# Order of loads and of the first q products in a diffusion layer, with idle matmuls between

## The chip, the cores and the metric

One core of a Trainium2 chip. The metric is the device time of one execution in microseconds; lower is better. Five engines work side by side, each through its own queue in order: TensorE (PE; its weight loads are listed as PEld), VectorE (DVE), ScalarE (ACT), GpSimd (POOL) and SyncE (SP), which here issues nearly all DMA transfers.

## The reference

One layer of a transformer with adaptive norms, in fp32, on 128 context tokens and 512 latent tokens (640 in all), model width 1024:

- `mod = silu(cond) @ w_ada + b_ada` gives, for each of two condition vectors (context, latent), six vectors of 1024: shift, scale and gate for the mixer, and the same for the FFN.
- `h = rms(x, norm_mix) * (1 + sc1) + sh1`.
- `h @ w_in` is cut into q (512 columns), k and v (128 each) and three blocks of 512 for a gated short convolution.
- Attention on normed, rotated q and k; the convolution beside it; both normed, concatenated and put through `w_out`; a gated residual.
- The same modulation for a SwiGLU FFN of 2816 with a gated residual.
- Outputs: both token sets, and k and v of the context tokens.

Only the part up to `h @ w_in` for the q columns is touched by the change.

## The kernel before

All matmuls that need fp32 accuracy are done as three products of rounded parts: a value is split into a high part (`hi`, rounded to the fast fp32r form) and a low part (`lo = value - hi`), and `mm3` (lines 150 to 153) adds hi·hi, hi·lo and lo·hi. `split` (146 to 148) rounds on ScalarE and subtracts on VectorE. The split of the modulated tokens is `hH`, `hL`; that of the weights `wh`, `wl`.

**The first stage** (to about 63 us) makes `h` for all tokens and the q products. Model width is cut into eight blocks k of 128. For the stage these things are needed:

- `x_norm(t)` (`r` in the list, 470 to 475): for token tile t of 128 tokens, ScalarE squares and sums, VectorE makes `ms` (line 159), GpSimd takes the power -0.5 (161), VectorE scales x (475).
- `xT_do(t)` (`x`): eight turns (transposes) of x on TensorE into PSUM, and two copies of 512 columns out of it into `xT`, on ScalarE or VectorE as `XTE` says. For the first `XB` tiles both halves lie in one double PSUM tile, for the others in two single ones.
- `ada1_mm(k)` (`a`): the adaLN product for block k, eight small matmuls with the condition vectors (`cp`, 32 columns, of which two are used) as the stationary side. `cp` is set to zero on GpSimd (332); its two live columns are copied on VectorE (369) from `cs`, which comes from a turn of the SiLU of the conditions (362 to 366). VectorE copies the result out (`res`, 418).
- `ada1_mod(k)` (`m`): four tiny matmuls on `res` and then three small VectorE instructions (399, 400, 403) give scale `modA` and shift `modB` of block k.
- `h_do(k, cc)` (`h`): ScalarE makes `hF = modA * xT + modB` for the 512 latent tokens, VectorE for the 128 context tokens, then `split` makes `hH` and `hL`.
- `load_split` (`w`): the split of a loaded pair of q weight blocks (1024 columns).
- `q_mm(k, t)` (`q`): three matmuls of 512 columns that add block k to the q product of token tile t; five PSUM banks hold the sums over all k.

The order is written out. `P1PRE` is a list of these steps that is run first; while it is traced, VectorE, ScalarE and GpSimd keep exactly its order (`pre_order`), and so does TensorE (`pe_order`, from ahead of it to the end of the kernel). It ends with modulated blocks 0 and 1 and all q products of k = 0. Then a loop over k from 1 runs `P1SEQ`: modulation of k+1, `h` of k+1, adaLN product of k+2, and the five q products of k. In the loop the other engines are ordered by the planner of the language, by its own costs and by program order.

**Loads.** SyncE issues them. `LOADS` gives the first ones: 0 is the next x tile (512 KB), a positive number that many steps of the adaLN loads (a block k is two loads of two pieces, 1 MB, in two of the four `af` buffers; a third step hands the block over), -1 the next weight of the stream `order` (q weights, four pairs of 512 KB, then kv, then the convolution's). The buffers of block k come free when `ada1_mm(k-2)` is done. Further weights are issued when a product asks for its own (`W`, 252 to 261): it loads up to `AHEAD` = 3 places further. SyncE's order is the planner's.

**After it** follow the kv products, attention with the convolution between, the output projection and the FFN; TensorE's order in them is written out too (`SEQ`). They are not edited.

Of the kernel before, what the change touches and what calls it, by code (L numbers as in the profile page):

```python
# [30 lines left out]
EPS = 1e-6  # L31
CG = 32
SOQ = [0, -300, -300, -300]
P1SEQ = 'm h a 0 1 2 3 4'
P1PRE = ('r0 r1 r2 x0 r3 x1 v0 x2 a0 w0 x3 m0 r4 h00 a1 q02 q01 x4 q00 m1 h01 h10 a2 q03 h11 p0 q04 c0')
XB = 3
XTE = [0, 1, 0, 1, 1, 1, 0, 1, 1, 0]
SEQ = ('k1 c0 q4 k4 C0 k0 K4 Q4 q0 a0 F1 k2 a1 K0 t0 k3 t1 o0 K1 F1 Q0 o1 K2 F1 K3 F1 S0.0 F1 F1 S0.1 '
# [16 lines left out]
AOP = 9  # L55
# [18 lines left out]
AO = 6  # L74
# [6 lines left out]
AHEAD = 3  # L81
OSQ = 2
AFB = 4
LOADS = [0, 0, 0, 0, 2, 1, -1, 0, 3, 3, 2, 2]
O_Q, O_K, O_GB, O_GC, O_U = 0, 512, 768, 1280, 1792


def build(ctx, tc, x_prompt, x_sample, c, cache_k, cache_v, c_ctx, norm_mix, norm_ffn, w_ada, b_ada,
# [3 lines left out]
    act, dve, pool, pe, sp = nc.scalar, nc.vector, nc.gpsimd, nc.tensor, nc.sync  # L92
# [23 lines left out]
    def T(tag, shape, dt=F32, bufs=1):  # L116
        seq[0] += 1
        return pools[where.get(tag, "A")][1].tile(list(shape), dt, tag=tag, bufs=bufs, name=f"{tag}_{seq[0]}")

    def PB(shape=(P, 512), dt=F32, tag="t"):  # L120
        seq[0] += 1
        if kept.get(tag):
            w = kept[tag].pop()
            n = 1
            for y in shape[1:]:
                n *= y
            w = w[:, :n] if tag != "s" else w
# [12 lines left out]
    def f32(ap):  # L140
        return ap.bitcast(F32)
# [4 lines left out]
    def split(hi, lo, src):  # L146
        act.activation(hi, src, AF.Copy)  # L147
        dve.tensor_tensor(lo, src, f32(hi), ALU.subtract)  # L148
# [81 lines left out]
    deferred = []  # L230
    in_pre = [False]

    def load_split(e, wf):
        key, src, ph, ring, gain, _ = e
        a, b = src.shape[1], src.shape[2]
        wh = T(ring + "h", (P, a, b), F32R, WHB)
        wl = T(ring + "l", (P, a, b), F32R, WHB)
        if gain is None:
            with early(SOQ[key[1]] if key[0] == 'q' else SOW):
                split(wh, wl, wf)  # L240
        else:
            for i in range(a):
                g = vec[:, gain + i:gain + i + 1]
                act.activation(wh[:, i], wf[:, i], AF.Copy, scale=g)
                dve.scalar_tensor_tensor(wl[:, i], wf[:, i], g, f32(wh[:, i]), ALU.mult, ALU.subtract)
        e[5] = (wh, wl)

    def load_next(later=False):
        load(order[stream_at[0]], later)
        stream_at[0] += 1  # L250

    def W(key):
        p = place[key]
        while not in_pre[0] and stream_at[0] < len(order):
            nxt = order[stream_at[0]][0][0]
            ahead = AO if nxt == "o" else AOP if nxt in ("g", "u", "op") else AHEAD
            if stream_at[0] > p + ahead or order[stream_at[0]][2] > phase[0]:
                break
            load_next()
        assert order[p][5] is not None, key  # L260
        return order[p][5]
# [33 lines left out]
    for gi, grp in enumerate(GROUPS):  # L295
# [5 lines left out]
        for j in range(2):  # L301
            for i0 in range(0, len(grp), 2):
                n = len(grp[i0:i0 + 2])
# [3 lines left out]
                        plan(("ada", 5, 1, kp), wa[:, 2 * kp:2 * kp + 2, 5 * D + 512:6 * D], 2, "f")  # L307


    crow = T("crow", (16, P))  # L310
    sp.dma_start(crow[0:8, :], c[0].rearrange("(r q) -> r q", q=P))
    sp.dma_start(crow[8:16, :], c_ctx.rearrange("(r q) -> r q", q=P))
# [13 lines left out]
    ident = T("ident", (P, P))  # L326
# [4 lines left out]
    cp = T("cp", (P, KD, CG))  # L331
# [14 lines left out]
    def ada1_next(n):  # L346
        for _ in range(n):
            next(loads, None)
# [41 lines left out]
    modA = [T(f"modA{i}", (P, KD, 2)) for i in range(2)]  # L390
# [19 lines left out]
    def ada1_mm(k):  # L410
        while k not in ada1:
            ada1_next(1)
        rp = PB((P, 256), tag="c")
        for h, wf in enumerate(ada1[k]):
            for i in range(4):
                cond_mm(rp, 4 * h + i, wf[:, i].rearrange("p a b -> p (a b)"))
        res = T("res", (P, 256), F32, 2)
        dve.tensor_copy(res, rp)
        ada1[k] = res
# [8 lines left out]
    xT = T("xT", (P, KD, TOK))  # L428
# [21 lines left out]

    hF = {}

    def h_do(k, cc):
        if k not in hF:
            hF[k] = T("hF", (P, TOK), F32, 2)
        s = (slice(0, 512), slice(512, TOK))[cc]
        a, b = modA[0][:, k, cc:cc + 1], modB[0][:, k, cc:cc + 1]
        if cc == 0:
            act.activation(hF[k][:, s], xT[:, k, s], AF.Identity, bias=b, scale=a)
        else:  # L460
            dve.tensor_scalar(hF[k][:, s], xT[:, k, s], a, b, ALU.mult, ALU.add)
        if k == 0:
            split(hH[k][:, s], hL[k][:, s], hF[k][:, s])
        elif cc == 1:
            split(hH[k], hL[k], hF[k])

    pe_order = tc.manual_schedule(engines={mybir.EngineType.PE})
    pe_order.__enter__()

    def x_norm(t):  # L470
        junk = T2((P, D), mybir.dt.bfloat16)
# [37 lines left out]
    steps = {"r": x_norm, "c": late_consts, "w": lambda i: load_split(*deferred.pop(0)), "p": lambda i: rows2_load(), "x": xT_do, "v": lambda i: (vec_do, vec2_do)[i](), "m": ada1_mod, "a": ada1_mm}  # L509
    pre_order = tc.manual_schedule(engines={mybir.EngineType.DVE, mybir.EngineType.Activation, mybir.EngineType.Pool})  # L510
    pre_order.__enter__()
    in_pre[0] = True
    for x in P1PRE.split():
        k = int(x[1])
        if x[0] == "h":
            h_do(k, int(x[2]))
        elif x[0] == "q":
            q_mm(k, int(x[2]))
        else:
            steps[x[0]](k)  # L520
# [3 lines left out]
    sp.dma_start(ck, cache_k[0, 0])  # L524
    cv = T("cv", (P, NKV, HD))
    sp.dma_start(cv, cache_v[0, 0])
    for k in range(1, KD):
        ada1_next(3)
        for x in P1SEQ.split():
            if x == "m" and k + 1 < KD:  # L530
                ada1_mod(k + 1)
            elif x == "h" and k + 1 < KD:
                h_do(k + 1, 0)
                h_do(k + 1, 1)
            elif x == "a" and k + 2 < KD:
                ada1_mm(k + 2)
            elif x.isdigit():
                q_mm(k, int(x))
        if k == 2:
            vec2_do()  # L540

    qraw = [None] * NT
    for t in (CTX, 0, 1, 2, 3):
        qraw[t] = T("of", (P, 512), F32, NT)
# [751 lines left out]
```

## Time and profile before

| | |
|---|---|
| median of 3 runs | 761.24 us (761.2 to 762.45) |
| the profiled execution | 762.03 us, span in the profile 760.3 us |
| mean granted clock of TensorE in it | 0.995 |
| busy, share of span | PE 97%, DVE 74%, ACT 49%, POOL 6% |
| DMA | 84.5 MB, mean 111 GB/s; 291, 289, 258 GB/s in the first three fortieths (57 us) |

How to read the lines quoted below. A line of a group names the source line, the engine, the instruction, the tiles (out<-in), the shapes and the count; then busy time in total and mean ns of one; then the engine's idle time ahead of them and who ended it. A line of the timeline begins with the start and the duration in us. `[5.55 <-ACT t L473]` says the engine sat idle 5.55 us until that instruction released it. A line of the chain has the start, the time that the chain spent in it, and what it was. Matmuls overlap one another, so a duration is longer than the distance to the next.

### The profile page before, as it was taken

The page shows a single profiled execution, that of the slowest core. Times are in us where ns is not written, and L with a number is a line of the kernel's source. Part 1 is how long each engine was busy: PE and PEld are TensorE (multiplying, and loading weights), DVE is VectorE, ACT ScalarE, POOL GpSimd, SP SyncE. Part 2 cuts the span into 40 slices and gives each one's busy share as a digit, 9 for nine tenths or more (in the row PEclk, how much of TensorE's full clock was granted, in tenths as well). Part 3 has the DMA queues.
Part 4 walks back from the last instruction along what each step waited for, and adds up shares of the span by engine and source line. Part 5 has one row for each costly group of instructions (what it writes and reads, how often), then busy time and mean ns, then how long its engine had stood idle before and what let it go on. Part 6 is the DMA issues. An engine that isn't in the chain of part 4 may idle for free.

```text
span 760.3 us, 11889 instructions
## 1 busy us (share of the span) xinstructions
PE 738.2 (97%) x4580; PEld 663.4 (87%) x4580; DVE 559.1 (74%) x1009; ACT 373.6 (49%) x713; POOL 48.7 (6%) x77
## 2 busy tenths in 40 slices
PE   4999999999999999999999999999999999999997
PEld 3778988989999887799998789998889998899986
DVE  5556987676567799799879678875578866788653
ACT  5355776666555445865552135552125541255410
POOL 2104201011010130000000000000000000000000
PEclk9899999999999999999999999999999999999999
DMA  9994133423423453031325223223113132232312
GB/s 291 289 258 138 43 111 110 155 91 106 159 91 117 156 199 112 1 111 56 112 90 176 85 66 98 81 90 111 52 56 111 57 111 80 60 87 81 112 55 84
DMA packets 102349, 84.52 MB, mean 111 GB/s; under 512 B 4526, under 2 KB 82674, under 8 KB 102292
## 3 DMA queue, kind: packets, MB, share of 16 engines
q1 hardware_dynamic: 100980, 83.39, 36.1%
q8 instruction: 36, 0.59, 0.3%
q10 hardware_dynamic: 1056, 0.26, 0.2%
q14 instruction: 21, 0.17, 0.1%
q0 software_dynamic: 256, 0.11, 0.1%
HBM read 79.68 MB, written 2.75 MB: 108 GB/s over the span
## 4 chain that ended last, share of the span: by engine, by line
PE 80%; DVE 9%; ACT 3%; DMA 3%; issue 2%; SPq 1%; POOL 1%; POOLq 0%; DVEq 0%; ACTq 0%
PE pf L151 17%; PE pf L152 17%; PE pf L153 17%; PE pc L674 3%; PE pc L675 3%; PE pc L676 3%; PE ps L788 2%; PE po L831 2%; PE pt L814 2%; PE ps L151 2%; DMA af<-in_w_ada_dram 2%; PE pc L376 2%; PE ps L152 2%; PE ps L153 2%; POOL rs L161 1%
## 5 line engine op out<-in xcount | busy, mean ns | idle before, releaser
L147 ACT ACTIVATE wh<-wf 128x1024 fp32r<-128x1024 f32 (+1 forms) x76 | 64.2, 844 | 92.7 <-PE pf L153 63.1
L151 PE MATMUL pf<-wh,gT 128*128 128x512 f32 (+1 forms) x225 | 88.1, 391 | 0.0
L152 PE MATMUL pf<-wl,gT 128*128 128x512 f32 (+1 forms) x225 | 87.7, 390 | 0.0
L153 PE MATMUL pf<-wh,gT 128*128 128x512 f32 (+1 forms) x225 | 87.6, 390 | 0.0
L148 DVE TENSOR_TENSOR wl<-wf,wh 128x1024 fp32r<-128x1024 f32 (+1 forms) x42 | 49.3, 1174 | 28.1 <-ACT wh L147 25.2
L674 PE MATMUL pc<-hH,wh 128*128 128x320 f32 x192 | 61.1, 318 | 0.0
L676 PE MATMUL pc<-hH,wl 128*128 128x320 f32 x192 | 59.4, 309 | 0.0
L675 PE MATMUL pc<-hL,wh 128*128 128x320 f32 x192 | 59.3, 309 | 0.0
L151 PEld LDWEIGHTS pf<-wh,gT 128*128 128x128 f32 x225 | 42.2, 188 | 9.9 <-ACT wh L147 0.2
L152 PEld LDWEIGHTS pf<-wl,gT 128*128 128x128 f32 x225 | 42.2, 188 | 9.9 <-issue 0.2
L153 PEld LDWEIGHTS pf<-wh,gT 128*128 128x128 f32 x225 | 42.2, 188 | 9.8
L151 PE MATMUL pf<-T,wh 128*128 128x320 f32 x160 | 49.3, 308 | 1.5 <-ACT p L1129 1.5
L151 PE MATMUL pf<-T,wl 128*128 128x320 f32 x160 | 49.2, 308 | 0.0
L152 PE MATMUL pf<-T,wl 128*128 128x320 f32 x160 | 49.2, 308 | 0.0
L153 PE MATMUL pf<-T,wl 128*128 128x320 f32 x160 | 49.2, 308 | 0.0
L152 PE MATMUL pf<-T,wh 128*128 128x320 f32 x160 | 49.2, 308 | 0.0
L153 PE MATMUL pf<-T,wh 128*128 128x320 f32 x160 | 49.2, 307 | 0.0
L151 PE MATMUL pf<-B,wl 128*128 128x320 f32 x152 | 46.9, 308 | 0.0
L152 PE MATMUL pf<-B,wl 128*128 128x320 f32 x152 | 46.8, 308 | 0.0
L153 PE MATMUL pf<-B,wl 128*128 128x320 f32 x152 | 46.8, 308 | 0.0
L1208 DVE TENSOR_TENSOR dm<-pf,g 128x512 f32<-128x512 f32 (+1 forms) x41 | 27.7, 675 | 23.1 <-PE pf L153 23.1
L147 ACT ACTIVATE wl<-wf 128x512 fp32r<-128x512 f32 x34 | 21.4, 630 | 43.5 <-PE pf L152 36.8
(282 smaller groups left out, 2055.7 us busy)
## 6 DMA issues: line engine op xcount, KB each, us to landing
wf<-in_w_gate_up_dram SPq DMA_DIRECT2D x44, 512.0 KB, 4.0
aw<-in_w_ada_dram SPq DMA_DIRECT2D x24, 512.0 KB, 4.8
wf<-in_w_down_dram SPq DMA_DIRECT2D x20, 512.0 KB, 3.4
wf<-in_w_in_dram SPq DMA_DIRECT2D x18, 512.0 KB, 5.7
af<-in_w_ada_dram SPq DMA_DIRECT2D x32, 256.0 KB, 5.8
x<-in_x_sample_dram SPq DMA_DIRECT2D x8, 512.0 KB, 5.2
wf<-in_w_out_dram SPq DMA_DIRECT2D x8, 512.0 KB, 4.7
wf<-in_w_ada_dram SPq DMA_DIRECT2D x8, 512.0 KB, 3.8
```

The lines of the kernel that those rows point to most:

```text
L147: act.activation(hi, src, AF.Copy)
L148: dve.tensor_tensor(lo, src, f32(hi), ALU.subtract)
L151: pe.matmul(out, lh, rh, start=start, stop=False, skip_group_check=more)
L152: pe.matmul(out, lh, rl, start=False, stop=False, skip_group_check=more)
L153: pe.matmul(out, ll, rh, start=False, stop=stop, skip_group_check=more)
L376: pe.matmul(out[CG * g:CG * (g + 1)], cp[:, k], w, start=(k < 4), stop=(k >= KD - 4), skip_group_check=True)
L674: pe.matmul(acc, wh[:, k], hH[k][:, c0:c0 + n], start=(k == 0), stop=False)
L675: pe.matmul(acc, wh[:, k], hL[k][:, c0:c0 + n], start=False, stop=False)
L676: pe.matmul(acc, wl[:, k], hH[k][:, c0:c0 + n], start=False, stop=(k == KD - 1))
L788: pe.matmul(s2[:, g, :320], q, kk[:, v, P + g * 320:P + (g + 1) * 320], start=(i == 0), stop=(i == 1))
L814: pe.transpose(tp[:, i, h], u[3][h][:, kt * P:(kt + 1) * P], ident)
L1208: dve.tensor_tensor(dm, ps[:, :n], g2[cc][:, oc], ALU.mult)
```

## The change

- The list `P1PRE` is new. It begins with eight **idle products** (`d8`: `spin`, matmuls of `ident` with all 256 columns of `cp` into a PSUM tile that nobody reads); six more stand singly between its steps. It takes the q products of k = 0 by token tiles as their tokens get ready: `h` of block 0 is made in four parts (tiles 0 and 1, tile 2, tile 3, context). The q products of k = 1 are in the list as well, and `h` of block 2. The norms of x tiles 2, 3 and 4 stand later in it, between these.
- The loop starts at k = 2; its order is adaLN product of k+1, two q products, modulation of k+1, `h` of k+1, three q products. The adaLN product is thus one block ahead, not two.
- `h_do`: ScalarE rounds `modA * xT + modB` straight into `hH`; VectorE makes the fp32 `hF` for all tokens, and subtracts.
- `LOADS`: two x tiles, adaLN block 0, the first q weights, two x tiles, block 1, the context's x tile, block 2, the second q weights, block 3. The third and fourth q weights are issued in the loop behind the adaLN blocks 5 and 7; products no longer load q weights ahead.
- SyncE and TensorE keep the written order from the first transfer on, to the end of the loop.
- Two double PSUM tiles of x instead of three (`XB`), and other engines for its copies (`XTE`).

```diff
-P1SEQ = 'm h a 0 1 2 3 4'
-P1PRE = ('r0 r1 r2 x0 r3 x1 v0 x2 a0 w0 x3 m0 r4 h00 a1 q02 q01 x4 q00 m1 h01 h10 a2 q03 h11 p0 q04 c0')
-XB = 3
-XTE = [0, 1, 0, 1, 1, 1, 0, 1, 1, 0]
+P1SEQ = 'a 0 1 m h 2 3 4'
+P1PRE = ('d8 r0 r1 x0 v0 x1 d1 a0 d1 m0 d1 w0 h0a r2 d1 q00 q01 r3 x2 d1 h0b a1 q02 x3 d1 m1 h0c h1l q03 r4 q10 q11 x4 a2 '
+         'q12 q13 h04 h14 m2 w0 h2* q04 q14 p0 c0')
+XB = 2
+XTE = [0, 1, 0, 1, 0, 1, 0, 1, 0, 1]
...
-LOADS = [0, 0, 0, 0, 2, 1, -1, 0, 3, 3, 2, 2]
+LOADS = [0, 0, 2, 1, -1, 0, 0, 3, 0, 3, -1, 3]
...
-            ahead = AO if nxt == "o" else AOP if nxt in ("g", "u", "op") else AHEAD
+            ahead = AO if nxt == "o" else 0 if nxt == "q" else AOP if nxt in ("g", "u", "op") else AHEAD
...
+    sp_order = tc.manual_schedule(engines={mybir.EngineType.SP, mybir.EngineType.PE})
+    sp_order.__enter__()
...
+    HS = {"a": slice(0, 256), "b": slice(256, 384), "c": slice(384, 512), "l": slice(0, 512), "4": slice(512, TOK)}
+
+    def h_do(k, part):
         if k not in hF:
             hF[k] = T("hF", (P, TOK), F32, 2)
-        s = (slice(0, 512), slice(512, TOK))[cc]
-        a, b = modA[0][:, k, cc:cc + 1], modB[0][:, k, cc:cc + 1]
-        if cc == 0:
-            act.activation(hF[k][:, s], xT[:, k, s], AF.Identity, bias=b, scale=a)
-        else:
-            dve.tensor_scalar(hF[k][:, s], xT[:, k, s], a, b, ALU.mult, ALU.add)
-        if k == 0:
-            split(hH[k][:, s], hL[k][:, s], hF[k][:, s])
-        elif cc == 1:
-            split(hH[k], hL[k], hF[k])
-
-    pe_order = tc.manual_schedule(engines={mybir.EngineType.PE})
-    pe_order.__enter__()
+        for x in "l4" if part == "*" else part:
+            s, cc = HS[x], int(x == "4")
+            g, b = modA[0][:, k, cc:cc + 1], modB[0][:, k, cc:cc + 1]
+            act.activation(hH[k][:, s], xT[:, k, s], AF.Identity, bias=b, scale=g)
+            dve.tensor_scalar(hF[k][:, s], xT[:, k, s], g, b, ALU.mult, ALU.add)
+            if part != "*":
+                dve.tensor_tensor(hL[k][:, s], hF[k][:, s], f32(hH[k][:, s]), ALU.subtract)
+        if part == "*":
+            dve.tensor_tensor(hL[k], hF[k], f32(hH[k]), ALU.subtract)
+
+    def spin(n):
+        w = PB((P, 256))
+        for _ in range(n):
+            pe.matmul(w, ident, cp.rearrange("p a b -> p (a b)"), start=True, stop=True)
...
-    for k in range(1, KD):
+    for k in range(2, KD):
         ada1_next(3)
+        if k in (3, 5):
+            load_next()
         for x in P1SEQ.split():
             if x == "m" and k + 1 < KD:
                 ada1_mod(k + 1)
             elif x == "h" and k + 1 < KD:
-                h_do(k + 1, 0)
-                h_do(k + 1, 1)
-            elif x == "a" and k + 2 < KD:
-                ada1_mm(k + 2)
+                h_do(k + 1, "*")
+            elif x == "a" and k + 1 < KD:
+                ada1_mm(k + 1)
             elif x.isdigit():
                 q_mm(k, int(x))
-        if k == 2:
+        if k == 3:
             vec2_do()
 
+    sp_order.__exit__(None, None, None)
+    pe_order = tc.manual_schedule(engines={mybir.EngineType.PE})
+    pe_order.__enter__()
```

More of the change, by code (lines that the diff above doesn't have):

```diff
@@ L451, in build @@
     hF = {}
-    def h_do(k, cc):
+    HS = {"a": slice(0, 256), "b": slice(256, 384), "c": slice(384, 512), "l": slice(0, 512), "4": slice(512, TOK)}
+    def h_do(k, part):
         if k not in hF:
             hF[k] = T("hF", (P, TOK), F32, 2)
-        s = (slice(0, 512), slice(512, TOK))[cc]
-        a, b = modA[0][:, k, cc:cc + 1], modB[0][:, k, cc:cc + 1]
-        if cc == 0:
-            act.activation(hF[k][:, s], xT[:, k, s], AF.Identity, bias=b, scale=a)
-        else:
-            dve.tensor_scalar(hF[k][:, s], xT[:, k, s], a, b, ALU.mult, ALU.add)
-        if k == 0:
-            split(hH[k][:, s], hL[k][:, s], hF[k][:, s])
-        elif cc == 1:
-            split(hH[k], hL[k], hF[k])
-    pe_order = tc.manual_schedule(engines={mybir.EngineType.PE})
-    pe_order.__enter__()
+        for x in "l4" if part == "*" else part:
[11 more added lines that the diff above has]
+            pe.matmul(w, ident, cp.rearrange("p a b -> p (a b)"), start=True, stop=True)
     def x_norm(t):
@@ L507, in rows2_load @@
         pool.dma_start(rows2[8:20, :], conv_w[0].rearrange("w (r q) -> (w r) q", q=P))
-    steps = {"r": x_norm, "c": late_consts, "w": lambda i: load_split(*deferred.pop(0)), "p": lambda i: rows2_load(), "x": xT_do, "v": lambda i: (vec_do, vec2_do)[i](), "m": ada1_mod, "a": ada1_mm}
+    steps = {"r": x_norm, "c": late_consts, "w": lambda i: load_split(*deferred.pop(0)), "p": lambda i: rows2_load(), "x": xT_do, "d": spin, "v": lambda i: (vec_do, vec2_do)[i](), "m": ada1_mod, "a": ada1_mm}
     pre_order = tc.manual_schedule(engines={mybir.EngineType.DVE, mybir.EngineType.Activation, mybir.EngineType.Pool})
@@ L515, in build @@
         if x[0] == "h":
-            h_do(k, int(x[2]))
+            h_do(k, x[2])
         elif x[0] == "q":
```

## The prediction

> **What bounds the kernel now.** I read the page first, then the chain of waits in order of time, then the busy time by stretches, then the instructions of the first 75 us one by one, and last the groups by shape.
>
> ```profile
> span 760.3 us, 11889 instructions
> PE 738.2 (97%) x4580; PEld 663.4 (87%) x4580; DVE 559.1 (74%) x1009; ACT 373.6 (49%) x713; POOL 48.7 (6%) x77
> af<-in_w_ada_dram SPq DMA_DIRECT2D x32, 256.0 KB, 5.8
> ```
>
> TensorE is busy nearly throughout, so a gain must come from where it waits or runs at half clock. Only the first 63 us are edited. Two rows of the chain of waits in that part, and the stretches (busy us of each engine, granted clock, DMA share, GB/s), cut where the granted clock changed:
>
> ```profile
> 11.84 7.41 DMA af<-in_w_ada_dram
> ...
> 32.50 8.34 DMA af<-in_w_ada_dram
> ```
>
> ```profile
> core 0: us, PE busy (x) PEld busy (x) DVE busy (x) ACT busy (x) POOL busy (x), PEclk, DMA share, GB/s
> 8.30:11.70 3.40, 3.40 (x16) 3.22 (x16) 2.11 (x4) 2.43 (x5) 1.10 (x2) 1.00 1.16 309
> ...
> 15.10:18.50 3.40, 1.24 (x13) 0.71 (x12) 3.02 (x8) 2.14 (x5) 0.27 (x1) 1.00 1.20 294
> 18.50:21.90 3.40, 2.51 (x12) 1.44 (x13) 1.87 (x3) 1.13 (x2) 3.27 (x6) 0.50 1.20 290
> 21.90:25.30 3.40, 3.40 (x14) 2.91 (x13) 0.69 (x1) 0.23 (x1) 0.00 (x0) 0.50 1.20 283
> ...
> 34.20:62.90 28.70, 27.96 (x174) 20.86 (x174) 15.14 (x36) 13.06 (x16) 1.43 (x2) 1.00 0.93 262
> ```
>
> Up to 34 us the chain is paced by the adaLN loads and by 6.8 us at half clock; from 34.2 us TensorE is dense (27.96 of 28.70). So the end of the q products, about 62.7 us, is what has to move, and all behind it follows: the kv products start there and TensorE stays in its written order to the end.
>
> ```profile
> 33.76 0.50 PE L425 MATMUL pt<-sel,res 128*128 128x2 f32 x4
> 34.19 1.07 PE L376 MATMUL pc<-af,cp 128*32 128x256 f32 x16
> 34.49 0.16 DVE L400 TENSOR_TENSOR modA<-modt,nb 128x2 f32<-128x2 f32 x1
> ...
> 46.60 0.50 PE L151 MATMUL ps<-wh,hH 128*128 128x512 f32 x1
> ...
> 51.64 0.50 PE L151 MATMUL ps<-wh,hH 128*128 128x512 f32 x1
> ...
> 62.72 0.28 PE L151 MATMUL pc<-wh,hH 128*128 128x256 f32 x1
> ```
>
> From 46.60 to 51.64 is one turn of the k loop, 5.04 us: 15 q matmuls, an adaLN product (1.0) and a modulation (0.43, from 33.76 to 34.19). That leaves 0.24 for a q matmul, 0.70 for a token tile, 3.5 for a k.
>
> **The idle products at the head.** They read `ident` and `cp`; `cp` gets its last write from VectorE at L369. The rows of VectorE and TensorE there:
>
> ```profile
> 3.04 0.25 PE L364 MATMUL pt<-ident,crow 16*128 16x16 f32 x1 [3.04 <-ACT crow L362]
> ...
> 6.61 0.15 DVE L159 TENSOR_SCALAR ms<-ss 128x1 f32<-128x1 f32 x1 [5.55 <-ACT t L473]
> 6.68 0.36 DVE L371 TENSOR_REDUCE sel<-ident 128x32 f32<-128x128 f32 x1
> 6.96 0.16 DVE L366 COPY cs<-pt 128x16 f32<-128x16 f32 x1
> 7.16 0.18 DVE L369 COPY cp<-cs 128x16 f32<-128x16 f32 x1
> 8.11 0.15 DVE L159 TENSOR_SCALAR ms<-ss 128x1 f32<-128x1 f32 x1
> 8.25 3.62 PE L436 MATMUL ps<-ident,x 128*128 128x128 f32 x16 [4.96 <-DVE ms L159]
> 8.93 0.75 DVE L475 TENSOR_SCALAR x<-x,rs 128x1024 f32<-128x1024 f32 x1 [0.67 <-POOL rs L161]
> ...
> 12.00 1.09 PE L436 MATMUL ps<-ident,x 128*128 128x128 f32 x8
> ```
>
> The condition was turned by 3.3 us, yet its two copies stand in VectorE's queue behind the first `ms`, which waits for a square on ScalarE until 6.61. Harmless before: `cp` was first read at 13 us. Nothing in the diff touches that part of VectorE's order, so I take it that `cp` is again ready at 7.34, eight idle products start at 7.4, and the turns of the first x tile, which started at 8.25, stand behind them.
>
> The price of one idle product (256 columns, two passes):
>
> ```profile
> L376 PE MATMUL pc<-af,cp 128*32 128x256 f32 x128 | 9.4, 401 | 2.7 <-DMA af<-in_w_ada_dram 2.7
> ...
> L996 PE MATMUL pt<-aacc,ones x4: 592/592/592, 293.3 to 294.6; 128*128 128x512 f32 x4
> ```
>
> Four records from 293.3 to 294.6 are 0.43 a pass of 512 columns, so 0.43 a product of 256 columns at full clock; the low bound is L376's 16 passes in 1.0 us, 0.13 a product, four column groups side by side, which an idle product isn't; the high bound is two passes at their full 0.59, 1.2. I take 0.43, and 0.86 at half clock: the first 16 turns took 3.62, 0.23 each, and eight at 12.0 took 1.09, so the clock was half until some 11.7 after a busy stretch from 8.3. With the same edge, five products run cold to 11.7 and three warm: the eight end at 13.0. The first x tile is turned 4.75 later than before.
>
> **From there to the k loop**, in the new order, where VectorE, ScalarE and GpSimd keep the written order too. Durations:
>
> ```profile
> L148 DVE TENSOR_TENSOR wl<-wf,wh 128x1024 fp32r<-128x1024 f32 x8 | 9.9, 1236 | 2.9 <-ACT wh L147 2.9
> L148 DVE TENSOR_TENSOR hL<-hF,hH 128x640 fp32r<-128x640 f32 x7 | 5.8, 822 | 1.9 <-ACT hH L147 1.9
> L418 DVE COPY res<-pc 128x256 f32<-128x256 f32 x8 | 3.4, 420 | 0.7 <-PE pc L376 0.6
> L461 DVE TENSOR_SCALAR hF<-xT,modA,modB 128x128 f32<-128x128 f32 x8 | 2.7, 343 | 0.1
> L449 DVE COPY xT<-ps 128x512 f32<-128x512 f32 x4 | 2.6, 683 | 0.0
> L148 DVE TENSOR_TENSOR hL<-hF,hH 128x512 fp32r<-128x512 f32 x1 | 0.7, 693 | 0.1
> L148 DVE TENSOR_TENSOR hL<-hF,hH 128x128 fp32r<-128x128 f32 x1 | 0.3, 293 | 0.4 <-ACT hH L147 0.4
> ...
> L459 ACT ACTIVATE hF<-xT,modB,modA 128x512 f32<-128x512 f32 x8 | 6.5, 811 | 8.4 <-DVE modA L400 7.1 <-DVE ms L159 1.3
> ```
>
> VectorE's `hF` of 512 columns isn't shown: between L461's 0.34 and L475's 0.75, I take 0.5; of 256 columns 0.45, `hL` of 256 0.43. A modulation costs 1.1 from its weight load to `modA` (0.89 by 33.76 and 34.49, and 0.2 before). ScalarE's rounding straight from xT (0.81 for 512, at most that for less) runs beside VectorE's `hF` and costs the path 0.6 once at most; that it drops a second pass there is worth nothing, since ScalarE isn't late.
>
> - x0, bias, x1, one idle product, adaLN product 0: 13.0 + 1.1 + 0.2 + 1.1 + 0.4 + 1.0 = 16.8. `res` 17.3, `modA` 18.4.
> - VectorE next has the split of the q weights (1.24), then `hF`, `hL` of 256 tokens: 20.55. The third matmul of q(0,0) waits for that; q(0,1) ends 21.5.
> - Only now, behind that `hL`, comes `ms` of x2: 0.82 to its scaling (8.11 to 8.93), 0.75: x2 is turned from 22.2 to 23.3 (before: 12.0), though its load has long landed. What waits behind it on VectorE: x3's scaling (23.7), the xT copy (24.4), `h` of tile 2 (25.05), `res` 1 (25.5).
> - x3 25.6 to 26.7, xT 27.4, modulation 1 to 28.6, `h` of tile 3 29.25, `h` of k 1 (0.5 + 0.69) 30.45, x4's scaling to 32.0, its turns to 33.15, adaLN product 2 to 34.15, q(1,2), q(1,3) to 35.55, modulation 2 to 36.7, q weights split 37.95, `h` of k 2 (0.5 + 0.34 + 0.82) 39.6; the third matmul of q(2,0) waits for it. q(2,1) 40.6, modulation 3, three tiles: k 2 ends at 43.3.
> - k 3 to 6: four turns of 5.04, 20.2; the turn of the late vectors 0.25; k 7 3.5: 67.3.
>
> Against 62.7 that is **+4.6 us**. TensorE's own work would end at 61.6: 13.0 + 19.55 (five x tiles 5.45, bias 0.2, six idle products 2.6, three adaLN products 3.0, three modulations 1.3, ten q tiles 7.0) + 25.2 + 3.75. The other 5.7 us are its waits for VectorE above.
>
> What I cost at nothing: the loads in their new order. 283 to 309 GB/s (rows above) from 1.5 us bring x0, x1, adaLN 0 (2.1 MB) by about 9 us and all up to x4 (5.2 MB) by about 18, ahead of their users; the adaLN load of k+2 waits for product k and is used two turns, 10 us, later, against 5.8 to landing. So the two DMA waits of the chain do go; the time goes to VectorE's order instead. The last q and kv weights come behind the last adaLN load and are hidden by a turn; were they late, up to 1 us. In the k loop `h` is made one turn ahead: from the modulation 0.9 + 0.5 + 0.34 + 0.82 = 2.6, needed 3.6 behind it; a weight split (1.24) between could cost 0.2, twice.
>
> Made against the profiled execution: 760.3 of span and 1.7 around it are 762.0; 766.6 then. That execution stands 0.8 above the median of 761.24, so on the median's scale **765.8 us**.
>
> **The rivals.**
> 1. `cp` is copied early (VectorE takes L366 and L369 ahead of `ms`). For it: its inputs are there at 3.3; against it: the rows above. The products then run from 3.8: five cold and three warm end at 9.5, all behind is 3.5 earlier: +1.1, 762.3.
> 2. The other side, not slower: the waits are hidden, because VectorE's links fit beside TensorE's work. Place: between modulation 0 and k 3. Price: 5.7 us, end at 61.6, 760.1. It decides once the waits are under 1.1 us. For it: VectorE has only some 20 us of work in the 32 from 7.4; against it: its queue is in order, and each link above waits for the one before.
> 3. The idle products don't hold the clock. For it: 1.24 us busy of 3.4 (15.1 to 18.5) was followed by 0.50. Against it: these stretches held 1.00, and my emptiest has about 2:
>
> ```profile
> 38.90:42.30 3.40, 2.66 (x25) 1.66 (x25) 3.26 (x8) 2.25 (x3) 0.00 (x0) 1.00 1.13 306
> 73.00:76.40 3.40, 2.54 (x21) 2.25 (x22) 3.40 (x15) 2.99 (x8) 0.88 (x2) 1.00 0.14 41
> ```
>
> One or two stretches of 3.4 at half speed cost 1.7 to 3.4: 767.5 to 769.2, say 768.4. The Trainium skill ("TensorE: Matmul & The Clock Gate", Part 1: The HAM clock gate) has the clock fall only after a whole idle window of about 3.4 us. By that rule rival 3 could not occur, as no wait of mine is that long, and the time would stay 765.8. The trace doesn't agree: the window that was followed by 0.50 held 1.24 us of work. So the rival keeps a small chance.
>
> **How the numbers follow.** Forecast 0.54 (its own range 763 to 769, by the unshown costs and the edge of the clock, 12.5 to 14.2 for the eight products), rival 1 0.17, rival 2 0.20, rival 3 0.09. 0.2% is 1.5 us, about what a measurement of this kernel tells from no change. Slower: 0.52 of the forecast and all of rival 3, 0.61. Faster: 0.15 from rival 2 (with the copy part early it reaches 757) and 0.05 from rival 1: 0.20. The rest is 0.19. The range 758.5 to 769.5 leaves out the far ends of rivals 2 and 3.
>
> **What would show it.** Of after: the row of L369 at 7.2 and the first idle product at 7.4 (rival 1: 3.8); the first turns at 13.0; `ms` of x2 behind `hL` of the first 256 tokens and x2's turns at 22; TensorE waiting on `hL` and on `ms` rather than on DMA; no clock of 0.50 after 13 (rival 3: one); turns of 5.04 from k 3; the kv products starting at 67.3. I am wrong if these start before 64.2.

## The result, and the profile after

The kernel after takes **770.75 us** (median, 769.81 to 774.94) against 761.24 (760.55 to 762.45): a ratio of 1.0131 [1.0105, 1.0157], 9.5 us slower. I had forecast 765.8. The profiled execution is the longest of its five (774.94 us, span 773.2, mean clock 0.990); its landmarks up to 105 us are used below, and sums over the kernel go by medians. One execution of e3 below ran in a slower state (818.63 us, clock 0.849) and is left out.

The head went much as the working has it. TensorE's timeline of after:

```profile
7.45 6.73 PE L477 MATMUL pt<-cp,ident 128*128 128x256 f32 x16 [4.19 <-DVE cp L372]
14.02 1.04 PE L439 MATMUL ps<-ident,x 128*128 128x128 f32 x8
...
20.07 0.51 PE L152 MATMUL ps<-wh,hH 128*128 128x512 f32 x1
...
21.37 0.50 PE L154 MATMUL ps<-wh,hL 128*128 128x512 f32 x1 [0.35 <-DVE hL L469]
...
22.85 1.09 PE L439 MATMUL pt<-ident,x 128*128 128x128 f32 x8 [0.29 <-DVE ms L160]
...
45.25 1.07 PE L379 MATMUL pc<-af,cp 128*32 128x256 f32 x16
...
71.19 0.28 PE L152 MATMUL pc<-wh,hH 128*128 128x256 f32 x1
...
105.18 0.46 PE L801 MATMUL ps<-KA,qT 128*128 128x320 f32 x2
```

The idle products wait for `cp` until 7.45 and hold the first turns until 14.02; x2's turns stand behind `ms`. What the forecast has no row for is the distance between the last rows: the first attention scores of the latent tokens (105.18, before 92.96) come 34.0 us behind the kv products (71.19), before 30.2. The chain of waits of after there, and VectorE's row at its end:

```profile
53.36 6.79 DMA wf<-in_w_in_dram
60.17 1.07 ACT wh L148
...
63.27 0.50 PE ps L154
...
66.56 0.43 ACTq L571
67.02 8.52 DMA pr<-rope_s_dram
75.61 2.27 POOL tab L584 x8
77.90 0.22 DVE pl L610
```

```profile
77.35 0.22 DVE L610 TENSOR_TENSOR pl<-pc,tab 128x64 f32<-128x64 f32 x1 [2.15 <-POOL tab L584]
```

The same tables in the kernel before, GpSimd's and VectorE's timelines:

```profile
63.36 2.15 POOL L571 TENSOR_TENSOR tab<-pr,gnq 128x64 f32<-128x64 f32 x4 [1.98 <-DMA pr<-rope_s_dram]
65.48 1.16 POOL L571 TENSOR_TENSOR tab<-pr,gnk 128x64 f32<-128x64 f32 x4
...
66.59 0.35 DVE L597 TENSOR_TENSOR pl<-pc,tab 128x64 f32<-128x64 f32 x2
```

Before, the rotary tables (128 KB each) are made by 66.64 and their first reader starts at 66.59 with no wait. After, ScalarE issues their loads at 66.56 and 67.02. In its queue they stand behind the split of the last q weights, which landed only at 60.15, and behind the rounding of the last block, which waits for `modA` until 65.24. Against the kv products that is only 0.6 us later than before (57.49 there). What is longer is the way: they go beside the 512 KB loads of the kv and convolution weights, the second takes 8.5 us to land (before some 5.4: GpSimd waits for it until 63.36), and VectorE stands still for the tables until 77.35 and again until 77.90. TensorE waits behind it, first in after and then in before:

```profile
80.14 0.36 PE L631 MATMUL pt<-identr,osq 128*128 128x128 f32 x2 [3.10 <-ACT osq L623]
```

```profile
68.94 0.36 PE L618 MATMUL pt<-identr,osq 128*128 128x128 f32 x2 [0.37 <-ACT osq L610]
```

After this wait the granted clock is 0.50 from 81.83 to 85.25. That belongs to the 34.0 us too: where such a wait was followed by half clock (after, e2, e5, e10), the scores come 33.9 to 34.7 us behind kv, and where it wasn't (e3, e4), 32.4 and 32.6.

Two more things are in the profile of after. Its half clock, by stretches as in the prediction:

```profile
27.60:31.00 3.40, 2.49 (x11) 1.58 (x11) 2.12 (x8) 1.98 (x4) 0.00 (x0) 0.95 0.93 264
31.00:34.40 3.40, 3.40 (x13) 2.40 (x12) 1.57 (x3) 0.64 (x2) 2.49 (x4) 0.55 0.08 13
```

Two later stretches of half clock follow waits of TensorE: the one from 81.83, and 6.8 us from 238.85.

And, against the direction of the result, the last projection of the FFN is faster. By shapes, before and then after (min/median/max ns):

```profile
L152 PE MATMUL pf<-wl,gT x225: 276/394/398, 403.3 to 755.9; 128*128 128x512 f32 x108, 128*128 128x256 f32 x5
```

```profile
L153 PE MATMUL pf<-wl,gT x225: 283/389/398, 420.0 to 768.9; 128*128 128x512 f32 x108, 128*128 128x256 f32 x5
```

The change doesn't touch that code. The experiments on this come third below.

### The profile page after: what moved, and what is told of

Read it like the earlier page. It is cut to its first block, busy times and chain, and to the rows that moved or that the text cites. A ratio compares the mean times of both kernels' runs of the same rounds, so it can differ in the third digit from the quotient of the medians.

```text
span 773.2 us, 11964 instructions
## 1 busy us (share of the span) xinstructions
PE 747.9 (97%) x4608; PEld 671.2 (87%) x4608; DVE 562.9 (73%) x1021; ACT 371.3 (48%) x715; POOL 48.7 (6%) x77
## 4 chain that ended last, share of the span: by engine, by line
PE 80%; DVE 9%; ACT 3%; DMA 3%; issue 2%; POOL 1%; POOLq 0%; SPq 0%; ACTq 0%; DVEq 0%
PE pf L152 17%; PE pf L154 17%; PE pf L153 17%; PE pc L687 3%; PE pc L688 3%; PE pc L689 3%; PE ps L801 2%; PE pt L827 2%; PE po L844 2%; PE pc L379 2%; PE ps L154 2%; PE ps L152 2%; PE ps L153 2%; PE pt L477 1%; DMA pr<-rope_s_dram 1%
## 5 line engine op out<-in xcount | busy, mean ns | idle before, releaser
L148 ACT ACTIVATE wh<-wf 128x1024 fp32r<-128x1024 f32 (+1 forms) x76 | 64.0, 843 | 90.3 <-PE pf L154 61.5
L152 PE MATMUL pf<-wh,gT 128*128 128x512 f32 (+1 forms) x225 | 86.9, 386 | 0.0
L154 PE MATMUL pf<-wh,gT 128*128 128x512 f32 (+1 forms) x225 | 86.5, 384 | 0.0
L152 PE MATMUL pf<-B,wh 128*128 128x320 f32 x136 | 42.2, 310 | 0.0
```

Source lines behind the costliest of these rows:

```text
L152: pe.matmul(out, lh, rh, start=start, stop=False, skip_group_check=more)
L154: pe.matmul(out, ll, rh, start=False, stop=stop, skip_group_check=more)
```

## The experiments

Times are medians; ratios are to the kernel before, measured beside. Its medians beside the experiments were 761.24 to 762.18 us, so a difference of two runs' medians is good to about 1 us. "kv" is the start of the kv products and "scores" of the first attention scores of the latent tokens, both from the profile.

| kernel | x0 turned | kv | scores | us | ratio |
|---|---|---|---|---|---|
| before | 8.25 | 62.72 | 92.96 | 761.24 | 1 |
| after | 14.02 | 71.19 | 105.18 | 770.75 | 1.0131 [1.0105, 1.0157] |
| e1_rope_early | 13.14 | 69.18 | 99.8 | 767.47 | 1.0076 [1.0057, 1.0096] |
| e2_no_d8 | 8.22 | 66.75 | 100.7 | 767.55 | 1.0081 [1.0055, 1.0106] |
| e3_q_ahead | 13.38 | 69.50 | 101.9 | 768.27 | 1.0093 [1.0074, 1.0111] |
| e4_d8_on_ones | 9.09 | 65.07 | 97.7 | 764.21 | 1.0045 [1.0030, 1.0059] |
| e5_norms_early | 13.60 | 70.93 | 105.5 | 776.69 | 1.0198 [1.0166, 1.0230] |
| e6_three_mended | 9.54 | 66.41 | 97.0 | 762.38 | 1.0005 [0.9992, 1.0018] |
| e7_before_rope | 8.29 | 67.16 | 97.3 | 767.16 | 1.0069 [1.0047, 1.0092] |
| e8_all | 8.49 | 72.00 | 104.1 | 773.11 | 1.0146 [1.0120, 1.0172] |
| e9_before_layout | 8.35 | 62.61 | 92.9 | 757.76 | 0.9942 [0.9926, 0.9957] |
| e10_after_layout | 12.36 | 68.70 | 103.4 | 774.35 | 1.0164 [1.0143, 1.0185] |
| e11_layout_mix | 7.98 | 64.56 | 95.5 | 757.79 | 0.9945 [0.9925, 0.9965] |
| e12_before_idle | 9.02 | 68.67 | 99.3 | 763.04 | 1.0019 [1.0007, 1.0031] |
| e13_idle_same_order | 8.47 | 61.32 | 92.3 | 759.90 | 0.9971 [0.9955, 0.9986] |
| e14_idle_more | 7.95 | 62.03 | 92.5 | 759.07 | 0.9957 [0.9942, 0.9972] |

### One part of the change at a time

**e1_rope_early**: the rotary tables' loads leave ScalarE's queue and go to SyncE's, behind `cv`, into a tile of their own.

```diff
-    open_pool("B1", "left", "t2 tab selT identr ck cv")
+    open_pool("B1", "left", "t2 tab selT identr ck cv rope")
...
     sp.dma_start(cv, cache_v[0, 0])
+    rt = T("rope", (P, 2, NL, HD))
+    rc, rs_ = rt[:, 0], rt[:, 1]
+    sp.dma_start(rc, rope_c.rearrange("(t p) d -> p t d", p=P))
+    sp.dma_start(rs_, rope_s.rearrange("(t p) d -> p t d", p=P))
...
-    rt = T("pr", (P, 2, NL, HD), F32, PRB)
-    rc, rs_ = rt[:, 0], rt[:, 1]
-    act.dma_start(rc, rope_c.rearrange("(t p) d -> p t d", p=P))
-    act.dma_start(rs_, rope_s.rearrange("(t p) d -> p t d", p=P))
```

> The kernel after, with its two rotary tables loaded into a tile of their own right behind the cached keys and values (SyncE, about 28 us) and not by ScalarE's queue at 66.6 us. Theory A (three separate costs: a late head of the first stage, late q weights, late rotary tables): VectorE no longer waits for the tables, 3 to 4 us less than the kernel after's 770.75: about 767. Rival: ScalarE's copies of the q sums end the same wait a little later, so less than 1 us: 770.

Measured: 767.47 us, 3.3 less than after. Scores follow kv by 30.6 us again (after 34.0). The late tables are a cost of the change, and of about the size that this distance had shown (3.8 more than before).

**e2_no_d8**: `d8` is taken out of `P1PRE`; the six single idle products stay.

> The kernel after without the eight idle products at its head; the six single ones stay. Theory A: the first turns start at 8.3 us again, the head is 4 to 5 us earlier, the late weights and tables stay late by about the same against the q products: 766. Theory B (all follows from the late head): the late weights and tables go with it: 761 to 762. Rival C (the products pay by holding the clock): the turns and first products at half clock eat most of it: 769 to 771.

**e4_d8_on_ones**: the idle products read a constant instead of `cp`, two of 128 columns for one of 256.

```diff
-            pe.matmul(w, ident, cp.rearrange("p a b -> p (a b)"), start=True, stop=True)
+            for i in range(2):
+                pe.matmul(w[:, i * P:(i + 1) * P], ident, ones, start=True, stop=True)
```

> The kernel after with idle products of the same length that read the tile of ones (written at 1.0 us) in place of the condition columns (7.4 us). Theory A: they start at about 3.3 us, the first turns start by 9 to 10 us instead of 14, 3.5 to 4.5 us less: 766 to 767. Rival: what comes behind is held by loads or by VectorE anyway: 770 to 771.

Measured: without them 767.55 (3.2 less than after), on `ones` 764.21 (6.5 less). The first turns of both, e2 and then e4:

```profile
8.22 1.97 PE L439 MATMUL ps<-ident,x 128*128 128x128 f32 x8 [4.73 <-DVE ms L160]
...
10.42 1.97 PE L439 MATMUL ps<-ident,x 128*128 128x128 f32 x8
```

```profile
3.18 6.07 PE L478 MATMUL pt<-ones,ident 128*128 128x128 f32 x32
9.09 1.04 PE L439 MATMUL ps<-ident,x 128*128 128x128 f32 x8
...
15.17 0.50 PE L152 MATMUL ps<-wh,hH 128*128 128x512 f32 x1
```

Started at 3.18, they put the first turns off by only 0.9 us (9.09 for 8.22), and the turns go at full clock (1.04 for eight instead of 1.97). What made them costly was their operand: `cp`, made at 7.22 behind a wait for `ms`. In this order of the head, products on a constant take 3.3 us less than none (e4 against e2).

**e3_q_ahead**: q weights are again loaded up to three places ahead, and the two loads written into the loop are gone.

```diff
-            ahead = AO if nxt == "o" else 0 if nxt == "q" else AOP if nxt in ("g", "u", "op") else AHEAD
+            ahead = AO if nxt == "o" else AOP if nxt in ("g", "u", "op") else AHEAD
...
-        if k in (3, 5):
-            load_next()
```

> The kernel after with the q weights loaded ahead by the products as before (three places ahead), not one by one behind the adaLN blocks 5 and 7. Theory A: no wait for the last q weights (about 1.5 us), and the kv and convolution weights come before the rotary tables, so the tables land sooner too (1 to 3 us): 766 to 769. Rival: the adaLN loads are pushed back by 1.5 MB and TensorE waits for them: 771 or more.

Measured: 768.27, 2.5 less. The last weights are no longer waited for (kv 8.7 us behind block 7's product, in after 10.4), but adaLN block 5, now behind them, is later: its product starts at 50.56, 6.4 us after that of block 4 (44.14), where a turn takes 5.0. So a part of what one load gains the next one loses.

**e5_norms_early**: all four latent norms ahead of the first modulation. It takes VectorE's waits of the prediction (5.7 us) away by order, if order is what makes them.

```diff
-P1PRE = ('d8 r0 r1 x0 v0 x1 d1 a0 d1 m0 d1 w0 h0a r2 d1 q00 q01 r3 x2 d1 h0b
+P1PRE = ('d8 r0 r1 r2 r3 x0 v0 x1 d1 w0 a0 d1 m0 d1 h0a d1 q00 q01 x2 d1 h0b
```

> The kernel after with the norms of x tiles 2 and 3 straight behind those of 0 and 1, and the split of the first q weights ahead of the first modulation (as in the kernel before): VectorE does them while TensorE runs the idle products. Theory A (TensorE's waits in the head come from VectorE's written order): the wait for the split before the first q product and the one for the norm of x tile 2 go, 2 to 3 us less than the kernel after's 770.75: 768. Rival (VectorE is late by its amount of work, or the loads hold the head): 770 to 771.

Measured: 776.69. (Part of that is layout, below: against e10_after_layout, which has the same layout, it is 2.3 us slower, not 5.9.) ScalarE's timeline tells why it gains nothing:

```profile
13.05 1.06 ACT L482 ACTIVATE t<-x 128x1024 bf16<-128x1024 f32 x1 [5.05 <-DMA x<-in_x_sample_dram]
...
14.38 1.06 ACT L482 ACTIVATE t<-x 128x1024 bf16<-128x1024 f32 x1 [0.18 <-DMA x<-in_x_sample_dram]
...
15.44 1.06 ACT L450 ACTIVATE xT<-ps 128x512 f32<-128x512 f32 x2
```

x2 lands only at 13.05, and now the copies of x0 and x1 out of PSUM stand behind its square. The prediction's "its load has long landed" holds at 22 us, not at 12; the place of the norm in the change is near the place that the load allows.

### What is left when the losses are mended

**e6_three_mended**: e1, e4, and the third and fourth q weights loaded at k = 3 and 4 instead of 3 and 5.

> The kernel after with all three costs mended: idle products on the tile of ones, rotary tables early in their own tile, the last q weights issued behind adaLN block 6 and not 7; VectorE's order as in the kernel after. Theory A: from 764.2 (products on ones alone) the tables give back 2 us more (the stretch from kv to the first attention scores is 32.6 there, 30.6 with early tables) and the weights 1: 761 to 762, no change against the kernel before. Rival: the three share one slack, so little more than the first alone: 763 to 764.

Measured: 762.38, the time of before (1.0005). It starts its first q product at 15.62 (before 20.40), but by the start of k = 3 nothing of that is left: 41.67, and 41.55 before, with one adaLN product fewer done. Its waits in the k loop:

```profile
26.02 0.50 PE L154 MATMUL ps<-wh,hL 128*128 128x512 f32 x1 [0.60 <-DVE hL L469]
...
37.00 0.50 PE L154 MATMUL ps<-wh,hL 128*128 128x512 f32 x1 [0.96 <-DVE hL L471]
...
53.34 0.50 PE L154 MATMUL ps<-wh,hL 128*128 128x512 f32 x1 [0.52 <-DVE hL L471]
...
63.27 0.50 PE L154 MATMUL ps<-wh,hL 128*128 128x512 f32 x1 [0.57 <-DVE hL L471]
```

TensorE waits for VectorE's `hL`, as the prediction said it would, 0.5 to 1.0 us in these rows. kv start at 66.41, 3.7 behind before.

**e7_before_rope**: the edit of e1 on the kernel before. **e8_all**: e6, and a `P1PRE` with the norms first, modulation of all four latent tiles at once, two single idle products instead of six, and `XB = 3`.

> The kernel before with the rotary tables early in their own tile. Theory A: GpSimd's tables end at 66.64 there and VectorE's first use starts at 66.59, so there was next to no wait: 761 to 762, no change; the early tables are no gain of their own and only take back what the change cost. Rival: they are a gain in any kernel: 759 or less.

> The three mended, and a new order of the head: norms of x tiles 0 to 3 first, the weight split ahead of the adaLN product, x tiles 2 and 3 turned before the first modulation, the 512 latent tokens of block 0 modulated in one piece, one idle product each ahead of the first q products of blocks 0 and 1. Theory A: the waits on VectorE in the head shrink by some 3 us more: 757 to 760, faster than the kernel before. Rival: TensorE's amount of work up to the kv products sets the end and the idle products are added to it: 761 to 763.

e7: 767.16, slower, though scores follow kv by 30.2. The planner, which orders SyncE in the kernel before, moved other loads with the two small ones: the second q weights are issued at 30.53 (23.23 before), and the chain stands on them.

```profile
30.53 5.99 DMA wf<-in_w_in_dram
36.55 1.06 ACT wh L147
37.64 1.24 DVE wl L148
```

e8: 773.11. TensorE idles 6.87 us until 18.70 for VectorE's copies, and the q products start at half clock at 24.70. Both edits lose. (e7 and e8 have the layout of before, below, which is 4 us of e8's loss against e6.)

### The last projection

e6 has the time of before with kv 3.7 us late. In the records of both kernels, the same passes lie 3.7 us later in e6 at 320 to 400 us, and 0.3 later at 720: the loss is paid back in three stretches, and these are the passes `wh,gT` and `wl,gT`. The granted clock is 1.00 in both. The kernels fall into two groups, by where the built program puts `wh` and `wl` in each partition (bytes):

```
                            wh at    mod 128   gT mod 128   pitch of a pass, us
before, e5, e7, e8          19520    64        0            0.233
after, e1 to e4, e6         19584    0         0            0.227
```

The pitch is the mean of the 638 start-to-start distances under 0.3 us between the 645 passes of 512 columns. The weights are the moving side of these passes, `gT` the stationary one. The small tile `modt` (two buffers of 32 bytes) makes the difference: where the first modulation stands ahead of the first weight split in `P1PRE` (`m0 d1 w0`, in after), it is laid ahead of `wh`; otherwise behind.

**e9_before_layout** and **e10_after_layout** swap just that; three other small tiles (`ss`, `ms`, `rs`) move along. No instruction changes.

```diff
 (e9, on before)
+    T("modt", (P, 1, 2), F32, 2)
     steps = {"r": x_norm
 (e10, on after)
+    for tag in ("wh", "wl"):
+        T(tag, (P, 2, 4, P), F32R, WHB)
     steps = {"r": x_norm
```

> The kernel before, with one allocation of the small tile modt moved ahead of the first allocation of wh, as it stands in the kernel after: wh and wl begin 64 bytes later in every partition (offset 0 instead of 64 within 128 bytes), gT stays at 0. No instruction changes. Theory 'place of the weights': the passes of the last projection (wh,gT and wl,gT, 128x512) come every 0.2269 us instead of every 0.2333, 639 of them, so 4.1 us less: 757.2 us, everything up to 400 us unchanged. Rival 'order': the pitch follows something in the order of instructions that the change brought; then 761.2 us and a pitch of 0.2333.

> The kernel after, with one unused allocation of wh and wl ahead of the first of modt: wh and wl begin at offset 64 within 128 bytes, as in the kernel before; no instruction changes. Theory 'place of the weights': the pitch of the last projection goes from 0.2269 to 0.2333 us and the time from 770.75 to 774.9 us, and this is what the change costs without its accident of layout. Rival 'order': 770.75 us.

Measured: 757.76 and 774.35. The faster pitch moves with the layout, both ways. Rows of TensorE's timeline, the kernel before (48 passes from the first to the last of them) and e9 (51):

```profile
404.03 0.39 PE L152 MATMUL pf<-wl,gT 128*128 128x512 f32 x1
...
415.23 0.39 PE L152 MATMUL pf<-wl,gT 128*128 128x512 f32 x1
```

```profile
403.90 0.39 PE L151 MATMUL pf<-wh,gT 128*128 128x512 f32 x1
...
415.46 0.39 PE L151 MATMUL pf<-wh,gT 128*128 128x512 f32 x1
```

11.20 / 48 = 0.2333 and 11.56 / 51 = 0.2267 us. e9 beats both kernels: 0.9942 [0.9926, 0.9957].

**e11_layout_mix** lays `mH` and `mL` at offset 0 as well.

```diff
-        bb = T("cu", (P, TOK), F32, 2)[:, :512] if j else T("bb", (P, 512))
+        bb = T("cu", (P, TOK), F32, 2)[:, :512] if j else T("bb", (P, 520))[:, :512]
```

> As e9_before_layout, and the tile bb made 32 bytes longer, so that mH and mL (stationary in the mix projection, 216 passes wh,mH wl,mH wh,mL of 128x512) begin at offset 0 instead of 32 within 128 bytes. Theory 'both operands': the fast pitch needs moving and stationary tile at offset 0, so these passes also go from 0.2335 to 0.2270 us, 1.4 us less where they stand close together: 755.8 us. Rival 'moving operand alone': the stationary's place is no matter, the pitch stays 0.2335 and the time that of e9_before_layout, 757.2 us.

Measured: 757.79, no less than e9. The pitch of the mix projection's passes did go down, from 0.2332 in e9 to 0.2282 in the mean; so the place of the stationary tile counts too. But by the records that stage got less than 0.2 us shorter, so its passes aren't what sets its end.

### Do early idle products pay in the old order?

**e12_before_idle**: e9, with idle products on `ones`.

```diff
-P1PRE = ('r0 r1 r2 x0 r3 x1 v0 x2 a0 w0 x3 m0 r4 h00 a1 q02
+P1PRE = ('d8 r0 r1 r2 x0 r3 x1 v0 x2 a0 w0 x3 d2 m0 d2 r4 h00 a1 q02
```

> As e9_before_layout, and idle products on the constant ones tile: eight ahead of the turning of x0 and two each in two of TensorE's waits before the first q product; the order of all other work as in the kernel before. Theory 'the idle products pay when they are early': the turns of x0, x1 and x4 and the first nine q passes, at half clock in the kernel before (15.1 to 24.7 us), run at full clock: the first q product still waits for the adaLN block that lands at 19.25 us, the second k starts 2.5 to 3 us earlier, kv products at 60 us: 754.5 us. Rival 'loads bound the head': adaLN blocks land no earlier and the kv products start at 62 us or later: 757 us.

Measured: 763.04, 5.3 slower than e9. The clock is full to 31 us, but the planner had moved the cache loads ahead of weights and a weight split ahead of a copy on ScalarE, which stands 7.03 us for it:

```profile
27.55 1.06 ACT L147 ACTIVATE wh<-wf 128x1024 fp32r<-128x1024 f32 x1 [7.03 <-DMA wf<-in_w_in_dram]
28.52 0.58 ACT L447 ACTIVATE xT<-pt 128x512 f32<-128x512 f32 x1
```

So this run doesn't tell. **e13_idle_same_order** has fewer of them, and every other instruction of every queue in e9's order; **e14_idle_more** moves only the issues of `ck` and `cv`.

```diff
 (e13)
+P1PRE = ('d3 r0 r1 r2 x0 r3 x1 v0 x2 a0 w0 x3 d1 m0 d1 r4 h00 a1 q02
 (e14)
+P1PRE = ('d4 r0 r1 r2 x0 r3 x1 v0 x2 a0 w0 x3 d2 m0 d1 r4 h00 d1 a1 q02
```

> As e9_before_layout (757.8 us), and idle products on ones: three ahead of the turning of x0, one behind the turning of x3, one behind the modulation's turn of the first block; every other instruction stands in the order of e9_before_layout on every engine and DMA queue. Theory 'idle products pay when nothing else moves': the granted clock does not fall in 18 to 25 us, the six q passes at 0.43 us go at 0.235 and the turn of x4 at 1.0 instead of 1.9 us, together 2 to 2.5 us less: 755.4 us. Rival 'loads bound the head': the clock is full, but adaLN blocks and q weights then end the waits, and the kv products start within 0.5 us of 62.6: 757.8 us. Rival 'too few': the clock still falls, 757.8 us.

> As e13_idle_same_order with four idle products in front, two behind x3, one behind the modulation's turn and one ahead of the second adaLN product; beside them only the issues of ck and cv stand earlier in SyncE's queue. Theory 'idle products pay': full clock from 8 to 25 us, 755 us. Rival 'the queue': ck and cv stand ahead of adaLN blocks that the products wait for, and what is gained in clock is waited for again: 757 us or more.

Measured: 759.90 (757.97 to 763.21) and 759.07 (757.80 to 759.51), and e9 757.76 (756.25 to 758.71). kv start 1.3 and 0.6 us earlier than in e9, and the time is not less. In e13's profile the clock is still half from 19.06 to 22.48 (e9 from 19.27 to 26.1), in e14's it is full from 12.0 on. But there TensorE then waits for adaLN loads, 0.84, 0.59 and 0.49 us between 28 and 46 us, where e9's profile has no such wait: as e14's rival has it, what is gained in clock is waited for again. In e13's profiled execution the gain is gone at 225 us, at the end of attention (a row of the timeline, then two stretches):

```profile
225.56 0.60 PE L908 MATMUL pt<-ones,osq 128*128 128x1 f32 x4 [1.38 <-ACT osq L862]
```

```profile
223.50:226.90 3.40, 2.02 (x17) 1.94 (x16) 1.53 (x5) 2.58 (x6) 0.46 (x1) 1.00 0.00 2
226.90:230.30 3.40, 3.40 (x18) 3.40 (x17) 2.67 (x5) 1.90 (x5) 0.24 (x5) 0.55 0.00 0
```

VectorE had waited 2.65 us there for a 64 KB transfer (`es`; 1.24 us in e9), TensorE waits 1.38 us in turn, and the stretch after it runs at half clock. Against the same matmuls of before, e13 is 0.9 us early before that place and 1.8 late behind it. e9's profiled execution has no wait of TensorE there. The theory that early idle products pay by themselves isn't borne out in this order: they bring kv forward by about 1 us, and that doesn't reach the end. Whether the waits at 225 us come more often with them is open; e14's profile has one of 0.52 there without a fall of the clock.

## Why the prediction was wrong

The sign was right, the size was not: +9.5 where the sum said +4.6, outside the range.

- **The head, to block 4**: right in its landmarks. e10 runs the instructions of after, and its profiled execution kept the full clock up to 78.95 us: the idle products (5.52 us for eight, estimated 5.6), the first turns at 12.36 (13.0), x2's at 21.20 behind `ms` (22.2), block 4's product at 43.14 (43.3). The parts fit less well: the waits in e10's rows from 12.36 to 43.14 add up to 3.2 us, where I had 5.7, and TensorE's own work took that much longer; that the two misses cancel is luck. In the profiled execution of after nearly all eight ran at half clock (6.73) and the clock fell at 31 us: 45.25. The rows of e10:

```profile
7.00 5.52 PE L477 MATMUL pt<-cp,ident 128*128 128x256 f32 x16 [3.57 <-DVE cp L372]
12.36 1.04 PE L439 MATMUL ps<-ident,x 128*128 128x128 f32 x8
...
21.20 1.09 PE L439 MATMUL pt<-ident,x 128*128 128x128 f32 x8 [0.29 <-DVE ms L160]
...
43.14 1.07 PE L379 MATMUL pc<-af,cp 128*32 128x256 f32 x16
...
58.78 1.07 PE L379 MATMUL pc<-af,cp 128*32 128x256 f32 x16
...
68.70 0.28 PE L152 MATMUL pc<-wh,hH 128*128 128x256 f32 x1
```

- **Rival 1's price**, 3.5 us, is about what the head gains from products that start early: e4's first q product starts at 15.17, 3.3 us before e10's and 4.9 before after's. By medians e4 gives 6.5; its profiled execution also has no half clock behind the wait for the tables (2.79 us there).
- **Rival 2, waits that go away**: these waits are in the rows where they were forecast, and no other order of the norms took them away (e5, e8). With all else mended the written order still costs 4.6 us (e6 against e9, in one layout).
- **Rival 3, the clock**: it occurred in the profiled execution, beside the forecast and not in its place, and not once but three times (from 30.64, 81.83 and 238.85). A stretch with 2.49 of 3.4 us of work was followed by one at 0.55; in e10, where the stretches fell otherwise, 2.51 was followed by 1.00, and in e4 1.58 (69.32 to 72.73) was, too. So the busy time of a stretch doesn't tell in these records whether the clock falls; what does is open. The Trainium skill ("TensorE: Matmul & The Clock Gate", Part 1: The HAM clock gate) lets the clock fall only after a whole idle window. No such window is in these rows: 2.49, and in e13 2.02 us of work, stood ahead of half clock.
- **"What I cost at nothing: the loads in their new order"**: this step failed. Of the last weights I wrote "hidden by a turn; were they late, up to 1 us". From block 7's product to the kv products it is 9.9 us in e10 (58.78 to 68.70) and 10.4 in after, where a turn and a k are 8.54; so kv start at 68.70 for 67.3. In e6, with these weights issued earlier, it is still 9.4: 0.5 to 1.0 us go with their landing, and the rest is the wait for `hL` of the last block, which stands on VectorE behind a split of weights (e6's row at 63.27; in e3 no split stands there and it is 8.7). I had 0.2 for such a split. And the rotary tables, which ScalarE issues behind those weights' split, are nowhere in the working: 3.3 us by e1, and in e10 4.5 us from kv to the scores, 34.7 for 30.2. The argument was from when blocks are needed; it didn't ask which other queue stands behind a split that waits for a load, and what other loads are under way by then.
- **"All behind it follows"**: also failed, to the other side. The FFN's last projection gained 3.6 (e10 against after) to 4.4 us (e9 against before), because a tile of 64 bytes in all moved in the order of allocation. Without it the change costs 774.35 - 762.14 = 12.2 us (e10 against the kernel before beside it). In the profiles this adds up as 6.0 at the kv products, 10.5 at the scores and 12.2 at the end, the last 1.7 in small steps, most of them behind 220 us. So the miss of 4.9 us against the forecast would have been 7.6: that it is no larger is luck.
- Two small slips change nothing: 5.04 less 1.0 and 0.43 leaves 3.6 for a k, not 3.5, and TensorE's own work adds up to 61.5, not 61.6.

By medians, in one layout: 757.8 (e9); the written order +4.6 (e6); late idle products, late tables and late weights +8.4 (9.6 by the ratios), which singly give back 6.5, 3.3 and 2.5; 770.75. The three overlap. How the 4.6 divides between the `hL` waits and the adaLN product that comes a block later isn't settled.

## What to carry to other kernels

A filler must not read anything that is made late: give it a constant, and look up when its operand is written, behind what. When loads are reordered, follow each queue that stands behind a waiting instruction, the small transfers on other engines' queues above all; 128 KB issued beside bulk loads took 8.5 us here. When untouched code changes speed, compare the addresses of its operands before looking for a cause in the change.

## What the runs showed of the hardware

- **The place of a tile in the partition sets the pitch of a pass.** Passes of 512 columns of 4 bytes with a 128-column weight load each: 0.2333 us with the moving tile at offset 64 within 128 bytes, 0.2269 with moving and stationary tile both at 0; 2.8%, at the same granted clock of 1.00. With the moving tile at 0 and the stationary one at 32 (the mix projection in e9) it is 0.2332. Why, no run tells; 320-column passes, most of which have `wh` or `wl` as the stationary side, show no such difference (0.147 in before, after, e6 and e7).
- **A wait of one to two us can cost its double.** In e13 a wait of 1.38 us at the end of attention was followed by a stretch at 0.55 of the clock; in after, one of 1.77 us at the same place by two, at 0.50 and 0.52 (the stretches below). It need not: e4's wait of 2.79 us at 73.69 was followed by none. This is a good part of the spread between executions of one kernel: e13's two executions with a clock of 1.000 took 758.0 us, those with 0.990 to 0.993 took 759.4 to 763.2.

```profile
235.60:239.00 3.40, 1.63 (x14) 1.55 (x12) 2.07 (x5) 1.28 (x4) 0.00 (x0) 0.98 0.03 11
239.00:242.40 3.40, 3.40 (x15) 3.36 (x16) 0.85 (x2) 1.37 (x3) 0.70 (x5) 0.50 0.00 0
242.40:245.80 3.40, 3.40 (x16) 3.40 (x15) 2.14 (x5) 1.86 (x4) 0.00 (x0) 0.52 0.00 0
```

- **The planner of the language answers to small edits** (not hardware, but it cost as much). Two small loads (e7) or a few idle products (e12) changed the order of bulk loads that have nothing to do with them, and cost 5 us each.
